# A squared-ReLU MLP whose first product, too, is made of seven products of quarters

## The chip, the cores and the metric

One core of a Trainium2 chip runs the whole program. The metric is the device time of one execution in microseconds (us). TensorE is PE in the profile, VectorE DVE, ScalarE ACT, GpSimd POOL and SyncE SP; nearly all transfers are issued on SP, in program order.

## What is computed

Two layers of an encoder act on 1088 tokens of width 1024 (1024 of a prompt, 64 of a sample). Each layer has a mixer, a cross attention into 256 memory tokens, and an MLP, all with a root-mean-square norm ahead:

```
def rmsnorm(x, g):
    y = x32 * lax.rsqrt(jnp.mean(x32 * x32, axis=-1, keepdims=True) + EPS) * g
def cross_attn(h, mk, mv, w_q, w_o):        # 4 heads of 256
    q = (h @ w_q).reshape(B, L, N_MEM_HEADS, MEM_HEAD_DIM)
    pr = jax.nn.softmax(q k / 16);  return (pr v) @ w_o
def sq_relu_mlp(h, w_up, w_down):           # w_up 1024x4096, w_down 4096x1024
    return jnp.square(jax.nn.relu(h @ w_up)) @ w_down
...
x = x + cross_attn(rmsnorm(x, norm_cross[layer]), ...)
x = x + sq_relu_mlp(rmsnorm(x, norm_mlp[layer]), w_up[layer], w_down[layer])
```

## The kernel before

Tokens lie along the columns, features along the 128 partitions. They are two streams, s = 0 with 512 tokens and s = 1 with 576. All products are made to nearly fp32 accuracy from parts: each operand is split into a rounded high part and the low rest (`split`, L233/L236 and L186/L187: ACT rounds, DVE subtracts), and a product is three matmuls for each block of 128 rows: low times high, high times low, high times high. Weights come in blocks of 128 x 1024 (512 KB): SP loads one into a staging tile `st` (three of them, L174), ACT and DVE split it into `wp` (or `wd` in the second MLP product). A block is loaded as soon as a staging tile is free, and that is when the block two or three ahead has been split.

**Cross attention** (`cross`, then `project_back`) runs for s = 0 and then for s = 1: eight weight blocks `mq`, scores and values of four heads j, eight blocks `mo` which are added to x. The norm of the next stage is prepared within it (`prepared`): the squares of x are summed by PE, DVE scales the sum (L315), POOL raises it to the power -1/2 (L316, tile `rc`), and PE transposes `rc` (L326), from which the row `rb` is made. For s = 1 of the cross attention that is the norm of the MLP of s = 0.

**First MLP product** (`mlp_up`): 32 blocks of w_up. For each, three token blocks of 512, 288 and 288 columns get 24 matmuls each on the tokens times g, not yet normalised; DVE applies ReLU and `rb` on reading PSUM (L969), ACT squares into `u`. After two blocks POOL makes four differences of `u` (L992), and `u` with them goes to DRAM.

**Second MLP product** (`mlp_down`) is already seven products of quarters instead of eight: the token operands are those sums of `u`, and the weights are quarters of w_down and four sums of them, `sums`. `weights_sums` makes these during the first product, a sixteenth at a time: two loads of 512 KB into the one tile `quarters` (L943), four POOL additions of 128 x 512 (L947 to L950), a store of 1 MB to DRAM (L955).

In the first product SP and POOL keep the order of the program; elsewhere a scheduler arranges the instructions of each engine at build time. At run time each engine takes its instructions in order, and one that waits holds all that stand behind it.

## Time and profile before

| | us |
|---|---|
| median of 3 runs (lowest, highest) | 2772.16 (2770.36, 2772.91) |
| profiled execution: device time, span of its trace | 2772.14, 2770.3 |
| PE busy in the span | 2712.8 |
| cross attention, first layer, from 424 to 672: PE busy, POOL busy | 247.3, 15.9 of 248 |
| first MLP product, first layer, from 672 to 1053: PE busy, POOL busy | 379.8, 182.1 of 381 |

The second layer has the same stages, from 1776 to 2023 and from 2023 to 2404. Times in a timeline count from the start of the span. Busy PE is time with a matmul under way; PE is busy nearly throughout, so that a stage is as long as its matmuls and their waits. SPq is SP's queue of transfers: the time shown there is that of issuing one, not of the transfer.

### The profile page before, as it was taken

Reading aid. Unit: us, or ns where it says so; the run is one execution under the profiler, and the core shown is the slowest. Engines: PE = TensorE matmul, PEld = TensorE weight load, DVE = VectorE, ACT = ScalarE, POOL = GpSimd, SP = SyncE. Lnnn points to the kernel's source line nnn. Section 1 sums busy time; section 2 is a strip of 40 time slices with the busy share of each in tenths; the row PEclk is TensorE's granted clock in tenths of the full one; section 3 lists DMA queues with packets and bytes.
Section 4 is the critical chain, followed back from the end, with each engine's and each line's share of the span. In section 5 each row is a group of like instructions: output and inputs, shape, how many; then the busy total and the mean of one; then the engine's idle time right before and its main releaser. Section 6 shows DMA issues by size and latency. Waiting matters only on the chain. (4 is left out here: it accounts for less than half of the span.)

```text
span 2770.3 us, 44519 instructions
## 1 busy us (share of the span) xinstructions
PE 2712.8 (98%) x18280; PEld 2535.7 (92%) x18280; DVE 1393.6 (50%) x2328; ACT 1096.1 (40%) x1929; POOL 541.5 (20%) x486
## 2 busy tenths in 40 slices
PE   8999999999999999999999999999999999999998
PEld 7978998899999999999988899989999999999998
DVE  5596766564222226455457558566532222365453
ACT  5574555353221223333337348344432222243334
POOL 3200000000545442000003004000024555500000
PEclk9998999999999999999999999999999999999999
DMA  8722232322666668555421331323236666675452
GB/s 269 232 78 75 69 101 88 101 71 62 206 221 218 213 213 300 189 188 187 127 67 31 80 79 28 96 88 97 64 125 221 215 213 222 251 258 174 178 175 77
DMA packets 364368, 411.90 MB, mean 149 GB/s; under 512 B 45840, under 2 KB 267040, under 8 KB 364164
## 3 DMA queue, kind: packets, MB, share of 16 engines
q1 hardware_dynamic: 355268, 382.00, 41.8%
q0 software_dynamic: 8896, 27.06, 3.0%
q8 instruction: 143, 2.34, 0.4%
q14 instruction: 61, 0.50, 0.1%
HBM read 299.74 MB, written 109.39 MB: 148 GB/s over the span
## 5 line engine op out<-in xcount | busy, mean ns | idle before, releaser
L216 PE MATMUL mm<-hpH,wp 128*128 128x288 f32 (+2 forms) x5952 | 1422.7, 328 | 4.2 <-DVE U L543 2.6
L216 PEld LDWEIGHTS mm<-hpH,wp 128*128 128x128 f32 x5952 | 1015.5, 189 | 83.5 <-DVE U L543 2.9
L216 PE MATMUL mm<-hpL,wp 128*128 128x288 f32 (+2 forms) x2976 | 928.0, 328 | 2.2 <-DVE hpL L291 2.2
L216 PEld LDWEIGHTS mm<-hpL,wp 128*128 128x128 f32 x2976 | 562.3, 189 | 41.5 <-DVE hpL L291 3.1
L186 ACT ACTIVATE wp<-st 128x1024 fp32r<-128x1024 f32 x282 | 297.8, 1058 | 691.7 <-PE mm L216 434.7
L187 DVE TENSOR_TENSOR wp<-st,wp 128x1024 fp32r<-128x1024 f32 x282 | 344.8, 1224 | 271.3 <-ACT wp L186 266.7
L969 DVE SCALAR_TENSOR_TENSOR t<-mm,rb 128x288 f32<-128x288 f32 (+1 forms) x184 | 99.1, 539 | 507.9 <-PE mm L216 507.9
L992 POOL TENSOR_TENSOR u<-u 128x544 f32<-128x544 f32 x128 | 218.6, 1718 | 382.5 <-ACT u L974 380.0
L316 POOL TENSOR_TENSOR rc<-rc,mhalf 128x4 f32<-128x4 f32 (+1 forms) x21 | 23.4, 1122 | 986.9 <-DVE rc L315 986.9
L1041 PE MATMUL s<-uhl,wd 128*128 128x256 f32 x560 | 157.2, 281 | 4.6 <-DVE wd L187 4.6
L972 ACT ACTIVATE u<-t 128x512 f32<-128x512 f32 x64 | 40.4, 632 | 301.4 <-DVE t L969 301.4
L1042 PE MATMUL s<-uhl,wd 128*128 128x256 f32 x560 | 157.1, 281 | 0.0
L236 DVE TENSOR_TENSOR uhl<-ur,uhl 128x1088 fp32r<-128x1088 f32 x112 | 147.0, 1314 | 19.5 <-ACT uhl L233 19.4
L1043 PE MATMUL s<-uhl,wd 128*128 128x256 f32 x560 | 156.7, 280 | 0.0
L233 ACT ACTIVATE uhl<-ur 128x1088 fp32r<-128x1088 f32 x112 | 123.5, 1104 | 56.1 <-DMA ur<-u 54.0
L186 ACT ACTIVATE wd<-st 128x1024 fp32r<-128x1024 f32 x70 | 73.7, 1055 | 176.5 <-PE t L1043 142.8
L216 PE MATMUL s<-hpH,wp 128*128 128x288 f32 (+1 forms) x576 | 141.3, 330 | 0.0
L974 ACT ACTIVATE u<-t 128x288 f32<-128x288 f32 x128 | 55.9, 436 | 144.0 <-DVE t L969 144.0
L1041 PEld LDWEIGHTS s<-uhl,wd 128*128 128x128 f32 x560 | 105.9, 189 | 5.5 <-DVE wd L187 5.5
L1042 PEld LDWEIGHTS s<-uhl,wd 128*128 128x128 f32 x560 | 105.8, 189 | 0.0
L1043 PEld LDWEIGHTS s<-uhl,wd 128*128 128x128 f32 x560 | 105.6, 189 | 0.0
L216 PEld LDWEIGHTS s<-hpH,wp 128*128 128x128 f32 x576 | 98.0, 188 | 8.0 <-ACT hpH L233 0.3
(367 smaller groups left out, 4804.1 us busy)
## 6 DMA issues: line engine op xcount, KB each, us to landing
u<-u SPq DMA_DIRECT2D x32, 1904.0 KB, 6.7
ur<-u SPq DMA_DIRECT2D x112, 544.0 KB, 6.0
st<-in_w_up_dram SPq DMA_DIRECT2D x64, 512.0 KB, 4.2
quarters<-in_w_down_dram SPq DMA_DIRECT2D x64, 512.0 KB, 4.3
sums<-quarters SPq DMA_DIRECT2D x32, 1024.0 KB, 6.5
st<-sums SPq DMA_DIRECT2D x64, 512.0 KB, 5.5
st<-in_w_down_dram SPq DMA_DIRECT2D x48, 512.0 KB, 5.0
st<-in_w_mq_dram SPq DMA_DIRECT2D x32, 512.0 KB, 3.6
```

Source lines behind the costliest of these rows:

```text
L186: act.activation(wt[:, 0], st, AF.Copy)
L187: dve.tensor_tensor(wt[:, 1], st, f32(wt[:, 0]), OP.subtract)
L216: pe.matmul(ps, a, b, start=i == 0, stop=i == len(terms) - 1)
L233: act.activation(h, src, AF.Copy)
L236: dve.tensor_tensor(l, src, f32(h), OP.subtract)
L969: dve.scalar_tensor_tensor(t[:, :bn], ps[:, :bn], 0.0, nm.rb[:, b0:b0 + bn], OP.max, OP.mult)
L972: act.activation(slots[:, :, :256], t.rearrange("p (a b) -> p a b", a=2), AF.Square)
L974: act.activation(slots[:, b0 // 288, 256:], t[:, :bn], AF.Square)
L992: pool.tensor_tensor(u[:, to], u[:, a], u[:, b], OP.subtract)
L1041: pe.matmul(ps, wl, uh, start=first, stop=False)
L1042: pe.matmul(ps, wh, ul, start=False, stop=False)
L1043: pe.matmul(ps, wh, uh, start=False, stop=half == 1 and g == 3 and k == 1)
```

## The change

1. The first MLP product becomes seven products of quarters as well (class `Up`). Sixteen pairs of weight blocks give, for each stream, four quarters of 512 x 128 and three sums of them, and the halves of x give seven operands. A round is one pair of blocks with one stream: seven products of 12 matmuls of 256 columns (s = 0) or 288 (s = 1). There are 18 passes over weight pairs (two pairs are loaded twice) and 32 rounds a layer.
2. The weights' sums are made by POOL in the staging tiles (`weights`, four subtractions or additions of 128 x 512 for a pair), and each of the seven weight operands is split by ACT and DVE.
3. The token operands are normalised first (`operands`: for each stream sixteen DVE multiplications, four differences, seven splits) and stay in SBUF. Those of s = 0 are made during the last projection of the cross attention, those of s = 1 in the first two rounds of the first product.
4. The products are put together by DVE, which reads PSUM (seven additions a round), ACT takes ReLU and the square, POOL makes the four differences into the two single tiles `ss` and `sq`, and three stores a round take the place of the one store of two blocks.
5. `weights_sums` moves into the cross attention: two sixteenths after the scores of each head, in both streams, with its transfers on SP and its POOL work kept in the order of the program. There is still one tile `quarters`.
6. The second product's first weights lie in other tiles (`wd` for key[3] < 5, else `wp`), and its first tokens are loaded during the last round. `dynamic_dma_scratch_size` is halved.

The diff, cut to what the argument follows:

```diff
@@ cross, at the end of each head j
             scores(j)
             load_kv(j + 1, 0, 1)
+            for q in range(2):
+                weights_sums(l, 8 * s + 2 * j + q, p)
...
+    def weights_sums(l, q, p):
+        a = p.tile([128, 4, 512], F32, tag="quarters", name="quarters", bufs=1)
+        keep = tc.keep_in_program_order
+        for i in range(2):
+            keep(nc.sync.dma_start(a[:, 2 * i:2 * i + 2],
+                                   I["w_down"][l][256 * q + 128 * i:256 * q + 128 * i + 128]
+                                   .rearrange("p (h n) -> p h n", h=2)))
+        for to, one, two, op in ((3, 1, 3, OP.add), (1, 0, 1, OP.subtract), (0, 3, 0, OP.subtract),
+                                 (2, 2, 0, OP.subtract)):
+            keep(pool.tensor_tensor(a[:, to], a[:, one], a[:, two], op))
+        keep(nc.sync.dma_start(sums[l][q // 2][:, :, q % 2], a))
...
-    def mlp_up(l, norms, p, outer):
...
+    class Up:
...
+            self.streams = [0, 1, 0] + list(range(2, 16)) + [14]
+            self.rounds = [(0, 0), (1, 0), (1, 1), (2, 1)]
+            for k in range(3, 17):
+                self.rounds += [(k, 0), (k, 1)] if self.streams[k] != 14 else [(k, 0)]
+            self.rounds.append((17, 1))
...
+        def weights(self, w):
...
+            split(self.wp[j][:, 0], self.wp[j][:, 1], src)
+            if name == "A11":
+                pool.tensor_tensor(odd[:, hi], odd[:, lo], odd[:, hi], OP.add)
+                pool.tensor_tensor(odd[:, lo], even[:, lo], odd[:, lo], OP.subtract)
+                pool.tensor_tensor(even[:, lo], odd[:, hi], even[:, lo], OP.subtract)
+            elif name == "A12":
+                pool.tensor_tensor(even[:, hi], even[:, hi], even[:, lo], OP.subtract)
+            elif name == "S3":
+                self.load(k + 1, 0)
...
+            elif name == "S4":
+                self.load(k + 2, 1)
...
+            def finish(r):
...
+                act.activation(u, u, AF.Relu)
+                act.activation(u, u, AF.Square)
+                pool.tensor_tensor(t[0], u[:, 3], u[:, 0], OP.subtract)
+                pool.tensor_tensor(t[2], u[:, 2], u[:, 3], OP.subtract)
+                pool.tensor_tensor(t[1], u[:, 2], t[0], OP.subtract)
+                pool.tensor_tensor(t[3], t[1], u[:, 1], OP.subtract)
...
+            def hook(i):
+                r, m = up.slots[i]
+                if i == 3:
+                    nm1.columns()
+                elif i == 5:
+                    nm1.rows()
+                    for _ in operands(1, g, nm1, raw1, ops[1], operand):
+                        pass
```

**Three places in the order.** POOL, first layer, the end of the cross attention of s = 1, before (`kvst` are loads of memory keys and values, `o32` a sum of a head's outputs, `rc_6230` the power of the MLP norm of s = 0):

```order
L784 DMA kvst_5767<-kT0_3_801 128x512
L787 DMA kvst_5806<-in_cache_mem_v_dram 128x2x256
L787 DMA kvst_5869<-in_cache_mem_k_dram 128x2x256
L900 TENSOR_TENSOR o32_5798<-o32_5798 128x2x64
L784 DMA kvst_5944<-v0_3_867 128x512
L787 DMA kvst_6066<-in_cache_mem_v_dram 128x2x256
L900 TENSOR_TENSOR o32_6058<-o32_6058 128x2x64
L316 TENSOR_TENSOR rc_6230<-rc_6230,mhalf_107 128x4
L900 TENSOR_TENSOR o32_6175<-o32_6175 128x2x64
```

The same place after the change (L948 is the additions of `weights_sums`, L322 the power, now of `rc_6338`):

```order
L908 TENSOR_TENSOR o32_5894<-o32_5894 128x2x64
L792 DMA kvst_6056<-v0_3_867 128x512
L795 DMA kvst_6178<-in_cache_mem_v_dram 128x2x256
L948 TENSOR_TENSOR quarters_5974<-quarters_5974 128x512 x4
L948 TENSOR_TENSOR quarters_5982<-quarters_5982 128x512 x4
L908 TENSOR_TENSOR o32_6170<-o32_6170 128x2x64
L948 TENSOR_TENSOR quarters_6240<-quarters_6240 128x512 x2
L322 TENSOR_TENSOR rc_6338<-rc_6338,mhalf_107 128x4
L948 TENSOR_TENSOR quarters_6240<-quarters_6240 128x512 x2
L908 TENSOR_TENSOR o32_6303<-o32_6303 128x2x64
L985 TENSOR_TENSOR rd_6375<-rb_6374,ra_6373 128x1024
L948 TENSOR_TENSOR quarters_6248<-quarters_6248 128x512 x4
```

The power stood behind loads and small sums; now fourteen sixteenths and half of the fifteenth stand ahead of it (`rd` belongs to the operands of s = 0). The other power within the cross attention, of the norm of s = 1, has five sixteenths ahead of it. On PE, the transposes of `rc_6338` had 342 matmuls of `mo` behind them before the first product, and now have 363.

SP, the same stretch, before (the last blocks of w_mo, then those of w_up):

```order
L174 DMA st_6021<-in_w_mo_dram 128x8x128
L174 DMA st_6295<-in_w_mo_dram 128x8x128
L174 DMA st_6352<-in_w_mo_dram 128x8x128
L174 DMA st_6409<-in_w_mo_dram 128x8x128
L174 DMA st_6466<-in_w_up_dram 128x8x128
```

And after (L942 loads two halves of a sixteenth, L949 stores its sums, L173 and L1033 load weights):

```order
L173 DMA st_6133<-in_w_mo_dram 128x8x128
L942 DMA quarters_5982<-in_w_down_dram 128x1024 x2
L173 DMA st_6431<-in_w_mo_dram 128x8x128
L949 DMA sums0_6_90<-quarters_5982 512x1x512
L942 DMA quarters_6240<-in_w_down_dram 128x1024 x2
L949 DMA sums0_7_91<-quarters_6240 512x1x512
L942 DMA quarters_6248<-in_w_down_dram 128x1024 x2
L173 DMA st_6496<-in_w_mo_dram 128x8x128
L949 DMA sums0_7_91<-quarters_6248 512x1x512
L173 DMA st_6560<-in_w_mo_dram 128x8x128
L1033 DMA st_6746<-in_w_up_dram 128x8x128
```

The sixteenths follow one another, each load behind the store of the one before, since they share a tile; the loads of weights stand among them. The first sixteenth's loads come right behind the seventh block of `mq` of s = 0.

DVE in the first two rounds of the first product, before (L187 splits a weight block, L969 takes a product):

```order
L969 SCALAR_TENSOR_TENSOR t_6864<-s_6839,rb_6757 128x288
L969 SCALAR_TENSOR_TENSOR t_6892<-s_6867,rb_6757 128x288
L187 TENSOR_TENSOR wp_6951<-st_6637,wp_6951 128x1024
L969 SCALAR_TENSOR_TENSOR t_6920<-s_6895,rb_6757 128x288
L969 SCALAR_TENSOR_TENSOR t_6948<-s_6923,rb_6757 128x288
```

And after (L966, L986, L989 and L239 with a name such as `T2` make operands of s = 1; L239 with `wp` splits a weight operand; L1081 and L1090 put products together):

```order
L966 SCALAR_TENSOR_TENSOR rb_6902<-x1_7_128,gcol_109,rb_7003 128x288
L986 TENSOR_TENSOR rc_6900<-rb_6902,rc_6900 128x1152
L1081 TENSOR_TENSOR uC_6907<-s_7050,uC_6907 128x256
L989 TENSOR_TENSOR ra_6901<-rc_6900,rb_6902 128x1152
L239 TENSOR_TENSOR T2_6904<-rc_6900,T2_6904 128x1152
L239 TENSOR_TENSOR B21_6906<-rb_6902,B21_6906 128x1152
L239 TENSOR_TENSOR T1_6905<-rc_6900,T1_6905 128x1152
L1090 TENSOR_TENSOR uC_6907<-uC_6907,t_6910 128x256
L239 TENSOR_TENSOR wp_6812<-st_6750,wp_6812 128x512
L1081 TENSOR_TENSOR uC_6907<-s_7075,uC_6907 128x256
L239 TENSOR_TENSOR T4_7041<-ra_6901,T4_7041 128x1152
L239 TENSOR_TENSOR wp7_6360<-st_6875,wp7_6360 128x512
```

The splits of the last two weight operands of the second pass (`wp_6812`, `wp7_6360`) now have sixteen multiplications, three differences and five splits of operands, the last `T4`, ahead of them.

## Rows read from the trace of the kernel before

**Rows 1.** The page, busy time of the engines (share of the span, instructions).

```profile
PE 2712.8 (98%) x18280; PEld 2535.7 (92%) x18280; DVE 1393.6 (50%) x2328; ACT 1096.1 (40%) x1929; POOL 541.5 (20%) x486
```

**Rows 2.** Busy time by stretch; then granted clock, DMA share, GB/s.

```profile
424.00:672.00 248.00, 247.34 (x1569) 225.68 (x1568) 150.22 (x273) 113.89 (x231) 15.88 (x25) 1.00 0.29 85
672.00:1053.00 381.00, 379.80 (x2318) 348.61 (x2317) 97.85 (x140) 85.86 (x138) 182.08 (x123) 1.00 0.60 208
2410.00:2414.00 4.00, 4.00 (x23) 4.00 (x22) 0.00 (x0) 0.00 (x0) 3.92 (x4) 0.57 0.60 209
```

**Rows 3.** Timeline of PE, second layer: start, duration, engine, line, tiles, idle before.

```profile
2022.86 0.39 PE L216 MATMUL mm<-hpL,wp 128*128 128x512 f32 x1
...
2404.13 0.28 PE L1041 MATMUL s<-uhl,wp 128*128 128x256 f32 x1
...
2406.87 0.28 PE L1043 MATMUL s<-uhl,wp 128*128 128x256 f32 x1
2409.56 0.39 PE L1041 MATMUL s<-uhl,wp 128*128 128x256 f32 x1 [2.41 <-DVE wp L187]
```

**Rows 4.** Timeline of PE in the second product, 288 columns.

```profile
1103.08 0.29 PE L1041 MATMUL t<-uhl,wd 128*128 128x288 f32 x1
...
1106.25 0.29 PE L1041 MATMUL t<-uhl,wd 128*128 128x288 f32 x1
```

**Rows 5.** Timelines of POOL, SP and DVE over one unit of sums.

```profile
964.25 1.37 POOL L992 TENSOR_TENSOR u<-u 128x544 f32<-128x544 f32 x1
965.58 1.29 POOL L947 TENSOR_TENSOR quarters<-quarters 128x512 f32<-128x512 f32 x1
...
969.67 1.28 POOL L950 TENSOR_TENSOR quarters<-quarters 128x512 f32<-128x512 f32 x1
972.54 2.06 POOL L992 TENSOR_TENSOR u<-u 128x544 f32<-128x544 f32 x1 [1.59 <-ACT u L974]
...
973.97 0.52 SPq L955 DMA_DIRECT2D sums<-quarters  x1
980.15 0.82 SPq L943 DMA_DIRECT2D quarters<-in_w_down_dram  x2
...
972.16 1.22 DVE L187 TENSOR_TENSOR wp<-st,wp 128x1024 fp32r<-128x1024 f32 x1 [0.56 <-ACT wp L186]
```

**Rows 6.** The page's DMA issues (us to landing), and waits of SP's queue.

```profile
quarters<-in_w_down_dram SPq DMA_DIRECT2D x64, 512.0 KB, 4.3
sums<-quarters SPq DMA_DIRECT2D x32, 1024.0 KB, 6.5
st<-in_w_mq_dram SPq DMA_DIRECT2D x32, 512.0 KB, 3.6
...
SPq L943 <- DMA sums<-quarters: 169.3, 28, 7.5
```

**Rows 7.** Timelines of SP, POOL and PE, cross attention of the first layer.

```profile
422.24 0.37 SPq L174 DMA_DIRECT2D st<-in_w_mq_dram  x1
...
492.05 1.57 POOL L316 TENSOR_TENSOR rc<-rc,mhalf 128x4 f32<-128x4 f32 x2 [1.07 <-DVE rc L315]
...
624.92 1.04 POOL L316 TENSOR_TENSOR rc<-rc,mhalf 128x4 f32<-128x4 f32 x1 [12.71 <-DVE rc L315]
...
672.25 0.39 PE L216 MATMUL mm<-hpL,wp 128*128 128x512 f32 x1
```

**Rows 8.** Timelines of SP and POOL, cross attention of the second layer.

```profile
1773.06 0.37 SPq L174 DMA_DIRECT2D st<-in_w_mq_dram  x1
...
1975.53 1.03 POOL L316 TENSOR_TENSOR rc<-rc,mhalf 128x4 f32<-128x4 f32 x1 [12.71 <-DVE rc L315]
```

**Rows 9.** DVE by line and form, 424:672: count, busy, mean ns, idle before.

```profile
L187 DVE TENSOR_TENSOR wp<-st,wp 128x1024 fp32r<-128x1024 f32 x30 | 36.8, 1225 | 14.4 <-ACT wp L186 14.4
...
L813 DVE SCALAR_TENSOR_TENSOR q<-mm,rb 128x288 f32<-128x288 f32 x16 | 7.3, 455 | 12.6 <-PE mm L216 12.4
...
L236 DVE TENSOR_TENSOR hpL<-o,hpH 128x64 fp32r<-128x64 f32 x8 | 1.4, 216 | 0.0
```

More of the change, by code (lines that the diff above doesn't have):

```diff
@@ L119, in plan_mlp @@
     def plan_mlp(l):
-        for n in range(NFF):
-            plan.append(((("up", l), n), "n", cols(I["w_up"][l], n * 128, 128)))
+        stops.append(len(plan))
         w = I["w_down"][l]
@@ L192, in ahead @@
         def ahead(self, n=2):
-            while self.split < min(self.used + n, len(plan)):
+            while self.split < min(self.used + n, self.stop):
                 while self.load():
                     pass
-                if plan[self.split][1] == "s" and plan[self.split][0][3] >= 3 and self.more is None:
+                if plan[self.split][1] == "s" and self.more is None:
                     return
@@ L277, in __init__ @@
             self.count = 0
-            self.pair = Pair() if pair else None
+            self.pair = Pair() if pair and not plain else None
             self.out = None if pair else [hpp.tile([128, 4, NT2], F32, tag="hp", name="yT") for _ in range(2)]
-            if pair:
+            if pair or plain:
                 self.ss = nrm.tile([128, NT2], F32, tag="ss", name="ss", bufs=1)
@@ L287, in chunk @@
             g = gcol[:, c, self.g:self.g + 1]
-            if self.pair is not None:
+            if self.plain:
+                pass
+            elif self.pair is not None:
                 h, l = self.pair.at(c, 0, n)
@@ L755, in drain, with project_back @@
                 self.step()
-    def project_back(s, key, pair, queue=None, order=None, spare=0):
+    def project_back(s, key, pair, queue=None, order=None, spare=0, then=None):
         for n in range(8):
@@ L768, in project_back @@
                 queue.step(2)
+            if then is not None:
+                then(n)
     def cross(l, s, norm, p, then):
@@ L922, in cross @@
         then()
-        project_back(s, ("mo", l, s), o, order=[range(6), range(6, 8)], spare=4 - 2 * s)
+        return dict(s=s, key=("mo", l, s), pair=o, order=[range(6), range(6, 8)], spare=4 - 2 * s)
+    def weights_sums(l, q, p):
[9 more added lines that the diff above has]
+        keep(nc.sync.dma_start(sums[l][q // 2][:, :, q % 2], a))
     def load_u(us, p, m, g):
@@ L999, in mlp_down, with operands, scaled, parts @@
-    def mlp_down(l, us, first, last, p, outer):
-        W.more = p
+    def operands(s, g, nm, raw, ops, alloc):
+        h = WIDTH[s] // 2
+        def scaled(dst, k0, t):
+            for c in range(4):
+                dve.scalar_tensor_tensor(dst[:, c], x[s][k0 + c][:, t * h:t * h + h], gcol[:, k0 + c, g:g + 1],
+                                         nm.rb[:, t * h:t * h + h], OP.mult, OP.mult)
+        def parts(b):
+            if b not in ops:
+                ops[b] = alloc(b)
+            split(ops[b][:, 0], ops[b][:, 1], raw[b])
+        scaled(raw["B11"], 0, 0)
+        yield
+        scaled(raw["B12"], 0, 1)
+        yield
+        dve.tensor_tensor(raw["T1"], raw["B12"], raw["B11"], OP.subtract)
+        parts("B11")
+        yield
+        scaled(raw["B22"], 4, 1)
+        yield
+        scaled(raw["B21"], 4, 0)
+        yield
+        pool.tensor_tensor(raw["T3"], raw["B22"], raw["B12"], OP.subtract)
+        dve.tensor_tensor(raw["T2"], raw["B22"], raw["T1"], OP.subtract)
+        parts("T2")
+        yield
+        dve.tensor_tensor(raw["T4"], raw["T2"], raw["B21"], OP.subtract)
+        for b in ("B21", "T1", "T4", "B22", "T3"):
+            parts(b)
+            yield
@@ L1003, in mlp_down @@
+    def mlp_down(l, us, ready, last, p):
         steps = [(m, h) for m in range(7) for h in range(2)]
-        ready = {(0, g): t for g, t in enumerate(first)}
         banks = {}
@@ L1048, in mlp_down @@
                         g = 4 * after[1] + c
-                        ready[after[0], g] = load_u(us, outer, after[0], g)
+                        ready[after[0], g] = load_u(us, p, after[0], g)
                     if end:
                         next(finish, None)
-        W.more = None
     class Window:
@@ L1368, in attend, with prepared @@
                     self.step(t)
-    def prepared(s, g):
-        norm = Norm(s, g)
+    def prepared(s, g, plain=False):
+        norm = Norm(s, g, plain=plain)
         for c in range(KC):
```

280 lines of the change are left out of this document (194 added, 86 removed).

## The prediction

> **What bounds the kernel now.** I read the busy times first: PE works for 2712.8 us of the span [rows 1], so only fewer or shorter matmuls shorten the kernel, and any wait of PE lengthens it. Then the stretches: in the first MLP product PE is busy for 379.8 of 381 us at full clock; in the cross attention for 247.3 of 248 us, while POOL has 15.9 us of work there and DMA runs at 85 GB/s against 208 [rows 2]. Then the timelines, for the pace of a matmul and for what stands ahead of the two POOL powers (L316) in the cross attention, because PE waits for them in order.
>
> **The first product itself.** It takes 381.3 us, from 2022.86 to 2404.13 [rows 3]. After the change it has 16 pairs x 7 products x 12 matmuls = 1344 matmuls of 256 columns and 1344 of 288. Their pace is read from the second product, which has both: 23 steps from 2404.13 to 2406.87 are 0.119 us each [rows 3], 24 steps from 1103.08 to 1106.25 are 0.132 us [rows 4]. 1344 x 0.251 = 337 us.
>
> The other engines' work of one pair is to fit into 7 x 12 x 0.251 = 21.1 us. On DVE that is seven weight splits of half a 1224 ns split (L187) and fourteen additions of 455 ns (like L813) [rows 9], 10.7 us. On POOL it is four additions of 128 x 512 at 1.34 us [rows 5] and eight of half that width, 10.7 us. Both are hidden if their order lets them, which is the second rival below.
>
> The start is not hidden. The operands of s = 1 are made on DVE in the first two rounds, which have only products of s = 0. Up to the last weight split of the second round they are sixteen multiplications of 288 columns at 0.455 us, and three differences and five splits of 1152 columns at 1.224 x 1152/1024 = 1.38 us: 7.3 + 11.0 = 18.3 us [rows 9], with some 10 us of weight splits and additions between them. They begin when the norm of s = 1 is there, about 6 us into the stage. So that split ends 34 to 36 us in, while PE wants it before its fourteenth product, 13 x 12 x 0.119 = 18.6 us in. The wait is 10 to 20 us; I take 16. Product: 337 + 16 = 353 us, **28 us less per layer**.
>
> **The sums of w_down in the cross attention.** What they leave, the first product's POOL, was hidden there, so their removal brings nothing. What they enter is a chain. One unit before: both loads have landed 0.4 + 4.3 = 4.7 us after the first is issued [rows 6]; four additions take from 965.58 to 970.95; the store is issued at 973.97, and the next load leaves SP at 980.15, when the store has landed, 6.2 us later [rows 5]; the median store takes 6.5 us, and SP has waited for these stores 28 times [rows 6]. The next unit cannot overlap, for there is one tile. So a unit takes 4.7 + 5.4 + 6.2 to 6.5 = 16.3 to 16.6 us; I take 16.5.
>
> POOL beside DVE is slower: the L992 at 964.25 takes 1.37 us, the one at 972.54, beside an L187 of DVE on two SBUF inputs, 2.06 us [rows 5]. In the cross attention DVE groups with two SBUF inputs, ten from L187 (36.8 us) to the last (1.4 us) [rows 9], take 84 of 248 us, a third. Four additions that each lose 0.7 us in a third of the cases lose 0.9 us; as some fall into pauses of DVE, I take 0.4, hence **16.9 us a unit** (from 15.5, if nothing is lost and a store lands a microsecond sooner in the emptier stage, to 17.6).
>
> The Trainium skill (SBUF — State Buffer, section "SBUF: two separate sides") calls the port pair of GpSimd and DVE an exclusive lock, held for the whole instruction. The trace agrees in the two L992 above; by the lock alone every meeting would cost, some 0.9 us a unit, and the sum below would be about 2822.
>
> The first unit's load is issued behind the seventh mq block, at 422.6 [rows 7]. Unit k is then issued at 422.6 + 16.9 (k - 1). The order of POOL has two places where this matters:
> - The power for s = 1 stands behind the fifth unit's additions: 422.6 + 67.6 + 4.7 + 5.4 = 500.3 against 492.05 [rows 7]. PE is held by some 8 us. This is no cost of its own: the chain doesn't wait for PE, and PE meets it again at the next place.
> - The power for the MLP norm stands behind half of the fifteenth unit. It ends at 422.6 + 14 x 16.9 + 4.7 + 2.7 + 1.0 = 667.6, against 624.92 + 1.04 = 626.0 before [rows 7]: 41.6 us late. All of PE's remaining matmuls of mo queue behind its transposes. From that power to the first product it is 46.3 us now (672.25) [rows 7], and 21 more matmuls of 0.132 us make it 49.1: the first product begins at 716.7, 44.4 us later.
>
> The second layer is alike: 1773.06 to 1975.53 between the same two points is 202.5 us, as 422.24 to 624.92 is [rows 8, 7]. The clock falls after such a wait: behind the 2.4 us wait at 2409.56 the granted clock was 0.57 for four microseconds [rows 3, 2], about the lower level of 1.2 GHz, which costs some 1.7 us. I add 0.6, as the transposes and a few matmuls fill part of it: **45 us more per layer**. Weight blocks that stand behind units on SP still come in time: the seventh of mo follows the sixteenth unit's load at 422.6 + 15 x 16.9 = 676, and PE wants it six blocks after the power, past 700.
>
> **The start of the second product.** Its first operands are split behind the last round's work on DVE. Before, this place costs a wait of 2.4 us [rows 3] and a few more behind it; I add 1 us, from nothing to 5.
>
> **The sum.** Per layer -28 + 45 + 1 = +18, two layers +36. The profiled execution took 2772.1 us, the median of the runs is 2772.16, so the same: **2808 us**.
>
> **The rivals.**
> - *The chain is not late, and the fewer matmuls remain: faster.* POOL and DMA are nearly idle in the cross attention [rows 2], and a mq block lands in 3.6 us [rows 6]. If a store took no longer than the 1 MB of both loads, 4.7 us, a unit would be 14.8 us, the power 638.2, the first product 15 us late, a layer 12 us shorter: 2748. The point that decides is 15.6 us a unit, where 14 units save the 18 us. Against it: the median of the stores is 6.5 us over the whole program [rows 6]. 12 in 100. The Trainium skill (DMA: Bandwidth & Descriptors, section "Anatomy of one DMA — SWDGE (gpsimd) path") has 2.0 us and bytes/436 GB/s for a transfer, an estimate of 4.4 us for 1 MB either way; the store's 6.2 us disagrees, and by the page the end would be at about 2732.
> - *The first product is slowed all along.* `ss` and `sq` are single, so POOL's differences of a round wait until the three stores of the round before have landed, and the weight sums stand behind them on POOL. Stores are issued in the middle of the following round, some 5.7 us in, and land 6 to 7 us later: 12.4 us, against the 10 to 11 us of a round and the 2 us for ReLU and square. If this comes short by 1.5 us a pair, 15 pairs lose 20 us a layer: 2848. 14 in 100.
> - *POOL loses most of its meetings with DVE.* At 17.6 us a unit the power is late by ten microseconds more: 2828. 6 in 100.
> - *No change*, at 15.5 to 15.7 us a unit: 6 in 100.
>
> That the change does not do what it says can be left out: the order shows it on every engine.
>
> **Numbers.** The forecast has 62 in 100, with a range of its own from 2785 to 2830. Within 0.2% (5.5 us, about what a measurement of this kernel can tell from no change) 6 in 100; slower 62 + 14 + 6 = 82; faster 12. The range from 2768 takes in a unit of 15.5 us, to 2850 the slowed product; most of the faster case and the end of the slowed one are left out.
>
> **What would show it.** Right: PE waits at the transposes of `rc` for 25 to 45 us near 640 to 670 and again in the second layer, with POOL's additions of `quarters` waiting for loads ahead of it; the first product lasts about 353 us with a wait of 10 to 20 us some 18 us in; SP waits for stores of `sums` about 15 times in each cross attention. Wrong: units shorter than 15.6 us, or a first product that is longer than 365 us, or waits in each of its rounds.

## The result, and the profile after

| | before | after |
|---|---|---|
| median of 4 runs each (lowest, highest), us | 2771.26 (2767.77, 2772.91) | 2889.73 (2889.41, 2891.41) |
| after / before, 95% interval | | 1.043 (1.0412, 1.0449) |
| first layer, first product begins | 672.25 [rows 7] | 732.42 |
| second layer, first product begins | 2022.86 [rows 3] | 2146.61 |
| first layer, first product lasts, up to the second's first matmul | 381.3 | 380.5 |
| second layer, the same | 381.3 | 378.4 |
| second product, first and second layer | 346.3, 347.2 | 341.2, 344.1 |

The change costs 118 us where the forecast had 36. The cross attention is 60 us longer in the first layer and 68 us in the second, which begins 56 us later (1832.2 for 1776.0) and ends 124 us later; the first product, which should have paid for a part of it, gives back 1 and 3 us, and the second product 5 and 3.

The page after, span and busy times, which answers to [rows 1]:

```profile
span 2888.2 us, 47649 instructions
PE 2680.4 (93%) x19048; PEld 2547.6 (88%) x19048; DVE 1693.6 (59%) x2844; ACT 1247.5 (43%) x2113; POOL 772.2 (27%) x762
```

PE works 32 us less than before, and waits for 208 us of the span instead of 58. Two stretches of the first layer, the cross attention and the first product, in the columns of [rows 2]:

```profile
424.00:732.00 308.00, 258.24 (x1555) 231.71 (x1554) 187.02 (x290) 114.61 (x229) 114.79 (x93) 0.93 0.54 171
732.00:1113.00 381.00, 349.58 (x2709) 345.58 (x2707) 213.74 (x382) 160.19 (x233) 209.96 (x196) 0.97 0.43 134
```

In the first, PE waits for 50 of 308 us, where before it was 0.7 of 248. What PE waited for there (total us, times, longest):

```profile
PE t L867 <- DVE pr L856: 18.9, 6, 10.5
PE mm L219 <- DVE q L821: 13.7, 4, 4.1
PE t L332 <- POOL rc L322: 7.5, 1, 7.5
PE mm L219 <- DVE x L771: 4.0, 4, 2.8
```

No row names a weight split (`wp`): PE did not wait for weight blocks here. Most rows name DVE, which is not the cause of the longest waits. The timelines of POOL, ACT, DVE and PE around the longest wait, one after the other:

```profile
660.26 5.28 POOL L948 TENSOR_TENSOR quarters<-quarters 128x512 f32<-128x512 f32 x4 [11.72 <-DMA quarters<-in_w_down_dram]
665.51 0.45 POOL L908 TENSOR_TENSOR o<-o 128x128 f32<-128x128 f32 x1
675.22 2.65 POOL L948 TENSOR_TENSOR quarters<-quarters 128x512 f32<-128x512 f32 x2 [9.26 <-DMA quarters<-in_w_down_dram]
677.83 1.04 POOL L322 TENSOR_TENSOR rc<-rc,mhalf 128x4 f32<-128x4 f32 x1
...
665.99 0.40 ACT L236 ACTIVATE hpH<-o 128x64 fp32r<-128x64 f32 x2 [10.81 <-POOL o L908]
...
666.28 0.37 DVE L239 TENSOR_TENSOR hpL<-o,hpH 128x64 fp32r<-128x64 f32 x2 [10.57 <-ACT hpH L236]
...
668.64 1.09 PE L867 MATMUL t<-ident,pr 128*128 128x128 f32 x4 [10.47 <-DVE pr L856]
678.92 0.32 PE L332 MATMUL t<-ident,rc 128*128 128x128 f32 x1
```

Read from the top: POOL waits 11.7 us for a load of `quarters`; a sum of a head's outputs, 0.45 us long, stands behind the four additions; ACT waits 10.8 us for that sum, DVE 10.6 us for ACT, and PE 10.5 us for DVE's next work, `pr`. Then the fifteenth unit comes, and the power of the MLP norm behind half of it ends at 678.87, before it was 625.96 [rows 7]. PE's transposes of `rc` follow without a wait, since the chain had held PE already; the 7.5 us at L332 are those of the earlier power, at 503. Waits for `q` can have the same source: at 559.61 PE has waited 3.3 us for DVE, DVE 5.1 us for ACT, and ACT 6.7 us for a load of memory values that left POOL at 553.58, behind the eighth unit's additions.

The loads of the one tile, first layer (SP's issues: count, ns, first and last start):

```profile
L942 SPq DMA_DIRECT2D quarters<-in_w_down_dram x32: 328/424/1527, 420.7 to 687.0; - x32
```

The timeline of SP around the ninth unit, with a split on ACT and DVE:

```profile
541.46 0.82 SPq L942 DMA_DIRECT2D quarters<-in_w_down_dram  x2
553.66 0.52 SPq L949 DMA_DIRECT2D sums<-quarters  x1
554.27 10.25 SPq L173 DMA_DIRECT2D st<-in_w_mq_dram  x4
564.57 1.04 SPq L942 DMA_DIRECT2D quarters<-in_w_down_dram  x2
...
561.81 1.06 ACT L185 ACTIVATE wp<-st 128x1024 fp32r<-128x1024 f32 x1 [3.58 <-DMA st<-in_w_mq_dram]
...
562.90 1.23 DVE L186 TENSOR_TENSOR wp<-st,wp 128x1024 fp32r<-128x1024 f32 x1 [3.34 <-ACT wp L185]
```

From the first unit's loads to the sixteenth's, at 686.6, it is 265.9 us, 17.7 us a unit. The eighth takes 23.1: the ninth's loads stand on SP behind four weight loads. The last of the four leaves at 564.15, when DVE has freed a staging tile with the split at 562.90. That split waits through ACT for a block whose load had itself left SP only behind the eighth unit's store, at 554.27. The first product in slices of 20 us:

```profile
752.00:772.00 20.00, 9.42 (x64) 9.21 (x63) 16.92 (x24) 8.51 (x9) 9.32 (x5) 0.69 0.12 30
...
812.00:832.00 20.00, 20.00 (x162) 20.00 (x161) 9.91 (x19) 7.99 (x13) 11.42 (x11) 1.00 0.39 118
...
1072.00:1092.00 20.00, 16.14 (x116) 15.93 (x115) 10.77 (x21) 8.67 (x13) 11.68 (x12) 0.91 0.33 108
1092.00:1112.00 20.00, 14.79 (x107) 14.09 (x106) 13.86 (x21) 10.25 (x13) 8.10 (x8) 0.98 0.61 195
```

A full slice has 162 matmuls, 8.1 per us. The four slices up to 812 have 468, worth 57.8 of 80 us: 22 us lost. The twelve up to 1052 have 1903, 5 us lost; the rest, up to 1113, 378, 14 us lost. Without the 41 to 42 us lost the product would last some 339. What PE waited for in the first 80 us, and from 1052 to the second product's first matmul:

```profile
PE s L219 <- DVE wp L239: 12.3, 2, 10.6
PE t L332 <- POOL rc L322: 3.1, 1, 3.1
...
PE s L1257 <- ACT uhl L236: 5.0, 1, 5.0
PE s L219 <- DVE wp L239: 4.9, 3, 3.9
```

The 5.0 us are the wait for the second product's first tokens (`uhl`), which lies ahead of its first matmul and so within the 380.5.

### The profile page after: what moved, and what is told of

Its sections match the earlier page's. It is cut to its first block, busy times and chain, and to the rows that moved or that the text cites. A ratio compares the mean times of both kernels' runs of the same rounds, so it can differ in the third digit from the quotient of the medians.

```text
span 2888.2 us, 47649 instructions
## 1 busy us (share of the span) xinstructions
PE 2680.4 (93%) x19048; PEld 2547.6 (88%) x19048; DVE 1693.6 (59%) x2844; ACT 1247.5 (43%) x2113; POOL 772.2 (27%) x762
## 5 line engine op out<-in xcount | busy, mean ns | idle before, releaser
L219 PE MATMUL mm<-hpH,wp 128*128 128x288 f32 (+3 forms) x3008 | 731.8, 330 | 42.4 <-DVE q L821 27.6
L219 PEld LDWEIGHTS mm<-hpH,wp 128*128 128x128 f32 x3008 | 518.8, 190 | 86.3 <-DVE q L821 29.8
L219 PE MATMUL mm<-hpL,wp 128*128 128x288 f32 (+3 forms) x1504 | 473.4, 330 | 2.3 <-DVE hpL L297 2.2
L239 DVE TENSOR_TENSOR wp<-st,wp 128x512 fp32r<-128x512 f32 x252 | 215.9, 865 | 251.4 <-ACT wp L236 249.3
L219 PE MATMUL s<-T,wp 128*128 128x288 f32 (+1 forms) x2304 | 312.5, 294 | 37.0 <-DVE wp L239 36.7
L219 PEld LDWEIGHTS s<-T,wp 128*128 128x128 f32 x2304 | 301.2, 193 | 42.5 <-DVE wp L239 42.0
L219 PEld LDWEIGHTS mm<-hpL,wp 128*128 128x128 f32 x1504 | 288.8, 192 | 21.4 <-DVE hpL L297 3.2
L948 POOL TENSOR_TENSOR quarters<-quarters 128x512 f32<-128x512 f32 x128 | 182.0, 1422 | 347.6 <-DMA quarters<-in_w_down_dram 340.2
L322 POOL TENSOR_TENSOR rc<-rc,mhalf 128x4 f32<-128x4 f32 (+1 forms) x21 | 22.4, 1076 | 850.4 <-DVE rc L321 850.4
L219 PE MATMUL mm<-B,wp 128*128 128x256 f32 (+1 forms) x1536 | 204.6, 288 | 4.1 <-DVE wp L239 4.1
L219 PEld LDWEIGHTS mm<-B,wp 128*128 128x128 f32 x1536 | 197.2, 188 | 5.3 <-DVE wp L239 5.3
L239 DVE TENSOR_TENSOR uhl<-ur,uhl 128x1088 fp32r<-128x1088 f32 x112 | 143.9, 1286 | 17.8 <-ACT uhl L236 17.6
L1081 DVE TENSOR_TENSOR uC<-s,uC 128x256 f32<-128x256 f32 (+1 forms) x320 | 133.5, 432 | 11.6 <-PE s L219 5.0
```

What stands on the lines that cost most here:

```text
L219: pe.matmul(ps, a, b, start=i == 0, stop=i == len(terms) - 1)
L239: dve.tensor_tensor(l, src, f32(h), OP.subtract)
L322: pool.tensor_tensor(rc[:m, b0:b1], rc[:m, b0:b1], mhalf[:m, b0:b1], OP.pow)
L948: keep(pool.tensor_tensor(a[:, to], a[:, one], a[:, two], op))
L1081: dve.tensor_tensor(to, b, a, op)
```

## The experiments

Three explanations stood against one another for the 118 us: the chain (additions wait on POOL for loads, and short work that PE needs waits behind them), the transfers themselves, and the additions' own work, on POOL and beside DVE. For the first product the question was why it saved nothing. All medians, and ratios to runs of the kernel before on the same chip; not all kernels ran on one chip, so that differences of a few us between them show nothing:

| kernel | median, us | ratio (95%) |
|---|---|---|
| sums_alone | 2881.78 | 1.0399 (1.0381, 1.0417) |
| no_sums | 2757.10 | 0.9953 (0.9937, 0.9968) |
| no_adds | 2759.16 | 0.9966 (0.9949, 0.9982) |
| adds_only | 2795.84 | 1.0087 (1.0064, 1.011) |
| o32_dve | 2881.03 | 1.0396 (1.0379, 1.0412) |
| half_tiles | 2833.72 | 1.0218 (1.0192, 1.0244) |
| spread | 2824.43 | 1.0199 (1.0178, 1.022) |
| spread_kv | 2819.54 | 1.0175 (1.016, 1.019) |
| spread_sp | 2789.94 | 1.0069 (1.005, 1.0089) |
| spread_act | 2780.48 | 1.0037 (1.0022, 1.0051) |
| dve_adds | 2807.91 | 1.0128 (1.0103, 1.0153) |
| elsewhere | 2823.00 | 1.0183 (1.0167, 1.0198) |
| elsewhere_end | 2801.90 | 1.0112 (1.0097, 1.0127) |
| spread_start | 2825.10 | 1.02 (1.0182, 1.0218) |
| spread_end | 2808.15 | 1.0135 (1.011, 1.016) |
| no_sums_end | 2735.07 | 0.9875 (0.9851, 0.9899) |

### Which part costs

**sums_alone** is the kernel before with nothing but the move of `weights_sums` into the cross attention.

```diff
@@ cross, end of head j, in the kernel before
+            for q in range(2):
+                weights_sums(l, 8 * s + 2 * j + q, p)
@@ mlp_up
-            weights_sums(q)
```

> The kernel before with only weights_sums moved into the cross attention; the first product stays 32 blocks with the tokens scaled behind it. If what stands behind the units on POOL and SP costs the time (theory A), the cross attentions are 60 and 66 us longer, as in the changed kernel (678.9 to 732.4 in place of 626.0 to 672.3 at the end), and the kernel takes 2771 + 126 = about 2895 us. If the lengthening needs the new first product, whose operands are made in the last projection (theory B), it is at most the 45 us per layer of the power alone, some 2860, or near nothing.

The move alone costs 111 us. POOL at the end of the first layer's cross attention:

```profile
672.54 5.39 POOL L939 TENSOR_TENSOR quarters<-quarters 128x512 f32<-128x512 f32 x4 [9.07 <-DMA quarters<-in_w_down_dram]
677.88 1.04 POOL L316 TENSOR_TENSOR rc<-rc,mhalf 128x4 f32<-128x4 f32 x1
```

The same power, within 0.1 us of the same time as in the changed kernel: the new first product has no part in its lateness.

**no_sums** is the changed kernel without `weights_sums`; **no_adds** keeps its loads and stores, but not the additions; **adds_only** makes the additions on one cleared tile and keeps no transfer.

```diff
@@ no_sums (adds_only has the first of these edits too)
-                    src = sums[l][g][:, q]
+                    src = dram(w, 4 * g * 128 * D + q % 2 * 512, [[D, 128], [256 * D, 2], [1, 512]])
-            for q in range(2):
-                weights_sums(l, 8 * s + 2 * j + q, p)
@@ no_adds, in weights_sums
-        for to, one, two, op in ((3, 1, 3, OP.add), (1, 0, 1, OP.subtract), (0, 3, 0, OP.subtract),
...
-            keep(pool.tensor_tensor(a[:, to], a[:, one], a[:, two], op))
@@ adds_only, in weights_sums
-        a = p.tile([128, 4, 512], F32, tag="quarters", name="quarters", bufs=1)
+        if q == 0:
+            still[l] = p.tile([128, 4, 512], F32, tag="quarters", name="quarters", bufs=1)
+            pool.memset(still[l], 0.0)
+        a = still[l]
-            keep(nc.sync.dma_start(a[:, 2 * i:2 * i + 2],
...
-        keep(nc.sync.dma_start(sums[l][q // 2][:, :, q % 2], a))
```

> The changed kernel without weights_sums; the second product reads quarters of w_down where it should read their sums, so four of its seven weight operands are wrong, with as many loads and matmuls. Theory A: the cross attentions are as long as before but for a few us at their end (the x additions that wait beside the operands), the first product keeps its waits at the start and the end and gains nothing: 2889.7 - 2 x 58 = about 2770 to 2780 us. If the waits in the first product follow from the late cross attention (theory B), they fall away here too and the kernel takes about 2720 us.

> The changed kernel whose units load and store without the four additions between, so that the sums are plain quarters and the output is not the reference's. The transfers, their order on SP and the traffic stay, at some 11 us a unit; POOL has nothing that waits ahead of the powers, the o32 additions and the loads of keys and values. Theory A (what stands behind the additions on POOL costs the time): the cross attentions are at most 5 to 15 us longer than before, 2757 + 2 x 10 = about 2777 us. Rival (the transfers on SP hold the weight blocks, or the traffic holds the loads): above 2830 us.

> The changed kernel with the 64 additions of a layer kept at the end of each head on POOL, but on one tile that is cleared once: they wait for no load, and nothing is loaded or stored for them (the second product reads quarters of w_down where it should read their sums). Theory A (POOL's waits for transfers, with what is queued behind them): near the run without sums, 2757 to 2772 us. Rival (theory C: the additions themselves, which slow DVE and POOL beside each other and which the powers and loads stand behind, cost the time): 2800 us or more.

Between the changed kernel and no_sums lie 132.6 us. The transfers alone bring 2 of them, which is within the noise. The additions alone, which wait for no load, bring 39, where at most 15 were expected. The other 92 arise only where additions wait for loads: the chain. The windows of no_adds and of adds_only over the cross attention show the two ends, DMA at 217 GB/s with PE busy for 246.6 of 248 us in the one, PE at 234.3 in the other:

```profile
424.00:672.00 248.00, 246.55 (x1554) 224.12 (x1553) 164.90 (x292) 114.90 (x229) 22.93 (x29) 1.00 0.66 217
```

adds_only:

```profile
424.00:672.00 248.00, 234.33 (x1459) 211.36 (x1458) 181.60 (x280) 111.45 (x223) 91.94 (x74) 1.00 0.27 79
```

Part of the 39 us is DVE. Its groups by form, 424 to 672 (count, busy us, mean ns, idle before), in no_sums:

```profile
L856 DVE TENSOR_SCALAR pr<-pr,sm 128x256 f32<-128x256 f32 x32 | 9.8, 346 | 0.3
L239 DVE TENSOR_TENSOR ql<-q,qh 128x288 fp32r<-128x288 f32 x16 | 7.3, 454 | 2.7 <-ACT qh L236 2.6
L821 DVE SCALAR_TENSOR_TENSOR q<-mm,rb 128x288 f32<-128x288 f32 x16 | 7.3, 455 | 12.7 <-PE mm L219 12.5
L239 DVE TENSOR_TENSOR tp<-t,tp 128x512 fp32r<-128x512 f32 x16 | 10.3, 682 | 0.6 <-ACT tp L236 0.6
```

The same groups in adds_only:

```profile
L856 DVE TENSOR_SCALAR pr<-pr,sm 128x256 f32<-128x256 f32 x32 | 16.5, 557 | 0.3
L239 DVE TENSOR_TENSOR ql<-q,qh 128x288 fp32r<-128x288 f32 x16 | 14.5, 906 | 2.9 <-ACT qh L236 2.9
L821 DVE SCALAR_TENSOR_TENSOR q<-mm,rb 128x288 f32<-128x288 f32 x16 | 7.3, 455 | 8.8 <-PE mm L219 8.5
L239 DVE TENSOR_TENSOR tp<-t,tp 128x512 fp32r<-128x512 f32 x16 | 10.2, 679 | 0.6 <-ACT tp L236 0.6
```

Beside POOL's additions two groups that read only SBUF rise on average (`ql` 454 to 906 ns, `pr` 346 to 557), and those with an operand in PSUM (`mm`, `t`) stay as they were. The rise is that of a few operations: the median of `pr` is 347 ns in no_sums and 346 in adds_only, its longest 496 and 2026. The Trainium skill (SBUF — State Buffer, section "SBUF: two separate sides") has an exclusive lock, held for a whole instruction, between GpSimd and DVE operations that have two SBUF inputs or run in a two-port mode. These rows agree: `ql` has two SBUF inputs, the groups with an operand in PSUM have one. `pr` is held too; that it runs in such a mode is not shown.

### Is it the chain

**o32_dve** takes the sums of a head's outputs off POOL, **half_tiles** halves the unit and has two tiles, and **spread** has three half tiles, loads two units ahead, and a unit at each of several places of a head and of `project_back`.

```diff
@@ o32_dve
-                pool.tensor_tensor(o32[:, :, 0], o32[:, :, 0], o32[:, :, 1], OP.add)
+                dve.tensor_tensor(o32[:, :, 0], o32[:, :, 0], o32[:, :, 1], OP.add)
@@ half_tiles
-        a = p.tile([128, 4, 512], F32, tag="quarters", name="quarters", bufs=1)
+        a = p.tile([128, 4, 256], F32, tag="quarters", name="quarters", bufs=2)
@@ spread, class Sums
+            a = self.p.tile([128, 4, 256], F32, tag="quarters", name="quarters", bufs=3)
...
+            while len(self.tiles) < min(32, self.n + 3):
+                self.load()
@@ cross, project_back
+            ws.make()
```

> The changed kernel with only the small addition o32, for which PE waited 10.8 us in the last head (657.9 to 668.6), on DVE; the power of the MLP norm stays behind half of the fifteenth unit, and the chain of units with it. If the chain sets the end, as predicted, PE now comes earlier to the transposes of rc, waits there for the power at about 678, and the time is within 6 us of 2890. If the small waits added up to the 60 us (rival), the 10.8 us and the shorter ones behind o32 go in both layers: 2860 us or less.

> The changed kernel with the sums made in units of half the size in two tiles of half the size, the loads one unit ahead; POOL's work stays, its order too. Theory A with the transfers as the cause of the chain: a half unit then takes little more than the landing of its store, about 5 us, 10 in place of 17.8 us for a sixteenth, so that the last power is no longer late and the cross attentions are 5 to 15 us longer than before, not 63: 2889.7 - 2 x 52 = about 2785 us. Rival: POOL's additions beside DVE, or the order itself, cost the time whatever the transfers take: above 2850 us.

> The changed kernel with all its additions, in half units in three half tiles, set one by one between the halves of the queries, the heads and, for the first stream, the blocks of mo; a half unit's loads are issued two half units ahead, so that POOL finds its data landed. POOL has the same work, DMA the same bytes as in the run half_tiles (2834 us). Theory A: POOL no longer waits, and the cross attentions end within 5 to 10 us of the run without sums: 2765 to 2780 us. Rival (POOL's additions themselves, beside DVE, or their transfers slow the stage): 2820 us or more.

o32_dve gains only 9 us. One wait goes, and PE meets the chain at the next place, the power:

```profile
681.00 1.12 PE L332 MATMUL t<-ident,rc 128*128 128x128 f32 x4 [13.30 <-POOL rc L322]
```

No run has the powers off POOL too, so what they cost there by themselves is open.

half_tiles gains 56 us, about half of what was expected, as a half unit still takes some 7 us: SP itself is held, for 99.7 us by stores of `sums` between 424 and 680. Its timeline, where the next store stands behind a load that waits for the store before:

```profile
479.84 1.22 SPq L944 DMA_DIRECT2D quarters<-in_w_down_dram  x2
483.14 0.56 SPq L955 DMA_DIRECT2D sums<-quarters  x1
486.80 1.20 SPq L944 DMA_DIRECT2D quarters<-in_w_down_dram  x2
```

spread gains 65 us, where 110 to 125 were expected; it lies where the rival was put. One thing that is left is the order of POOL, now the other way round: additions stand behind a load of memory values that waits 22 us for DVE. They pile up from 494 to 543, and the next load of values leaves behind them at 543.11. ACT waits 12.9 us for that, DVE 11.6 us for ACT, and PE for DVE. POOL, and PE's wait:

```profile
491.34 0.72 POOL L795 DMA_DIRECT2D kvst<-in_cache_mem_v_dram  x1 [22.44 <-DVE v L239]
...
550.36 0.61 PE L219 MATMUL mm<-hpH,wp 128*128 128x288 f32 x1 [8.14 <-DVE q L821]
```

### Other places for the loads, the additions and the sums

All but elsewhere also leave out the single passes at the first product's end (spread_end, below), which are worth 16 us in spread. On top of spread, three have the head sums on DVE: **spread_kv** keeps the `kvst` loads on POOL in program order, **spread_sp** issues them on SP, **spread_act** on ACT (the latter two with the first head of s = 1 begun within the projection of s = 0). **dve_adds** makes the additions of w_down's sums on DVE. **elsewhere** takes the sums out of the cross attention: the first layer's are made in its mixer, the second layer's during the first layer's second product; **elsewhere_end** is the same without the single passes.

```diff
@@ spread_sp (spread_act: act.dma_start)
-                    pool.dma_start(st, kvd[l, which, j])
+                    tc.keep_in_program_order(nc.sync.dma_start(st, kvd[l, which, j]))
@@ dve_adds
-            keep(pool.tensor_tensor(a[:, to], a[:, one], a[:, two], op))
+                dve.tensor_tensor(a[:, to], a[:, one], a[:, two], op)
@@ elsewhere, second product
+                    if l == 0 and turn > 8 and turn % 8 < 6:
+                        ws.make()
@@ elsewhere, mixer
-            project_back(0, ("out", 0), mx.y[0], q)
+            project_back(0, ("out", 0), mx.y[0], q, then=ws.make)
```

> As spread_end (2808 us), with the loads of memory keys and values kept in the order of the program among the half units, and o32 on DVE. In spread POOL stood still for 22 us (469 to 491) behind such a load, which waited for its tile, and the half units of the first stream slid into the second. If that is where the rest of the time went (theory A again, with another waiting instruction), the cross attentions end within 10 us of the run without sums: 2808 - 2 x 20 = about 2765 us or less, at or below the kernel before. Rival: the additions cost time wherever they stand, by holding DVE; above 2795 us.

> As spread_end (2808 us), with the loads of memory keys and values on SP in the order of the program, those of the second stream's first head issued during the first stream's blocks of mo, and o32 on DVE: on POOL only the additions and the two powers are left. Theory A: no load waits behind an addition; 2745 to 2770 us, faster than the kernel before. Theory C: above 2790 us, with PE waiting for DVE all over the stage. A third way: SP's queue holds keys, values and weight blocks instead, with single waits of PE of 5 us or more, and 2780 us or more.

> As spread_sp (2790 us), with the loads of memory keys and values issued by ACT, where PE waited 3.1, 8.0, 2.4 and 1.2 us for them on SP in each layer. If those waits are SP's order, they go: 2790 - 2 x 12 = about 2766 us, no slower than the kernel before. Rival: ACT, which splits what it has just loaded, waits for the landing itself and holds what stands behind it: no gain or a loss.

> As spread_end (2808 us), with the additions of the sums on DVE in place of POOL: DVE gets 128 operations of 256 columns more in each layer, some 0.42 us each, 54 us, beside the 165 of 248 us that it is busy in the run without sums; POOL has none. If the additions cost through POOL and DVE holding each other and through POOL's queue, both are gone, and the cross attentions are at most 10 us longer than without sums: 2735 + 20 = about 2755 us, faster than the kernel before. Rival: DVE's own queue now waits for the loads, with the splits and products' results behind it: 2790 us or more.

> The changed kernel with all sums, made where POOL has next to nothing that PE waits for: those of the first layer in the mixer ahead (half units in three half tiles), those of the second layer in the first layer's second product (quarter units, 128 columns, in three tiles of 2 KB a partition), loads two units ahead. Theory A: nothing stands ahead of the powers and the loads in the cross attentions, which are as in the run without sums: 2757 to 2770 us. Rival: the 67 MB of loads and stores among the weight blocks on SP, or the additions beside a second product where DVE is half busy, give back as much: 2790 us or more.

> As elsewhere, without the second pass over pair 14 at the end of the first product. In the cross attention's spread version that gave 16 us (2824 to 2808 us) where 12 to 16 were expected. If those were the waits of two passes of one round each, the same 12 to 16 us come off here: 2742 to 2757 us, faster than both kernels. If the 16 us came from the changed cross attention or by chance, nothing does.

spread_kv misses: against spread_end it is 11 us slower, and PE now waits 9.0 us, up to 547.8, for a memory load that stands behind half units. With these loads off POOL the kernel comes to 2789.94 and 2780.48, the best with all sums, but 20 and 14 us above what was expected. The longest wait of spread_act is again one for DVE:

```profile
598.68 0.47 PE L872 MATMUL t<-ident,pr 64*128 64x64 f32 x2 [9.45 <-DVE tp L239]
```

dve_adds misses by 53 us and equals spread_end (2807.91 and 2808.15): DVE's own order then waits for the loads as POOL's did, 36.8 us in 23 waits between 424 and 700. elsewhere misses too, and elsewhere_end with it, though it is 21 us below elsewhere. Its cross attention is as clean as that of no_sums, but the sums cost as much where they went. The windows of the mixer and of the second product of the first layer, in elsewhere:

```profile
140.00:370.00 230.00, 202.97 (x1056) 176.11 (x1055) 191.44 (x316) 124.87 (x158) 126.21 (x124) 0.93 0.65 201
1080.00:1440.00 360.00, 337.71 (x2620) 335.39 (x2618) 185.63 (x199) 121.03 (x124) 186.21 (x261) 0.96 0.83 260
```

The same two stretches in no_sums:

```profile
140.00:340.00 200.00, 190.84 (x1034) 168.15 (x1033) 153.33 (x312) 122.42 (x155) 5.42 (x3) 0.97 0.26 76
1050.00:1380.00 330.00, 329.16 (x2622) 328.14 (x2621) 174.49 (x200) 119.36 (x123) 3.46 (x5) 1.00 0.53 183
```

Each stretch is 30 us longer for about the same matmuls. In the mixer DVE is busy for 191 us instead of 153, and PE waits for it; in the second product DMA is at 0.83 of its time and PE waits 12.9 us for the splits of tokens that land late.

### The first product

**spread_start** spreads the operands of s = 1 over the first rounds, one at a time; **spread_end** drops the two single passes at the end, so that each pair but those of the start is loaded once for both streams; **no_sums_end** is no_sums with the same end.

```diff
@@ spread_start, hook
-                    for _ in operands(1, g, nm1, raw1, ops[1], operand):
+                if 5 <= i < 14:
+                    next(make1, None)
...
+                elif i == 14:
+                    for _ in make1:
                         pass
@@ spread_end, no_sums_end
-            self.streams = [0, 1, 0] + list(range(2, 16)) + [14]
+            self.streams = [0, 1, 0] + list(range(2, 16))
...
-                self.rounds += [(k, 0), (k, 1)] if self.streams[k] != 14 else [(k, 0)]
-            self.rounds.append((17, 1))
+                self.rounds += [(k, 0), (k, 1)]
```

> As spread, with the operands of s = 1 made step by step between products 5 and 14, the weight splits among them, and POOL's difference T3 behind DVE's T4, which it held for 3.5 us. If the wait of 8 to 11 us about 24 us into the first product is due to the order on DVE, it shrinks by 4 to 6 us a layer: 8 to 12 us less than spread. Rival: DVE is simply full there (40 us of work against 20 us of products), the wait moves to the third round, and the time stays within 4 us.

> As spread, without the second pass over pair 14 at the end: 17 passes, the last two rounds being both streams of pair 15. If the waits near the end of the first product (1.7, 4.2, 0.7 and 1.1 us in the run without sums) come from two passes of one round each, whose weights must be summed and split in 10 us instead of 21, they go: 12 to 16 us less than spread over both layers. Rival: the second product then begins with a longer wait, since its first weights and tokens come later, and the time stays within 4 us of spread or rises.

> The run without sums (the second product reads quarters of w_down where it should read their sums) and without the second pass over pair 14. What the first product is worth by itself, without its last single pass: if the 16 and 21 us that this edit gave in two other kernels are the product's own, 2757 - 18 = about 2739 us; if they came with those kernels' cross attentions, 2750 us or more.

spread_start gains nothing. PE in the first rounds shows one long wait cut into several:

```profile
741.96 0.61 PE L219 MATMUL mm<-B,wp 128*128 128x288 f32 x1 [4.03 <-ACT B L236]
743.85 3.01 PE L219 MATMUL mm<-B,wp 128*128 128x288 f32 x11 [1.28 <-DVE B L239]
...
763.90 6.56 PE L219 MATMUL s<-T,wp 128*128 128x288 f32 x36 [2.46 <-DVE wp L239]
```

Two orders give the same time, as they would if the work were too much for these rounds; no run has less of it there. The end is another matter: spread_end is 16 us faster than spread, no_sums_end 22 us faster than no_sums, in two layers. The first product of no_sums in the first layer, in a window:

```profile
671.00:1049.00 378.00, 350.96 (x2707) 347.88 (x2705) 215.51 (x381) 160.78 (x233) 207.19 (x196) 0.97 0.43 134
```

The same of no_sums_end:

```profile
669.00:1032.00 363.00, 346.51 (x2706) 343.73 (x2706) 206.09 (x367) 154.72 (x224) 200.40 (x192) 0.98 0.43 137
```

The 15 us contain the wait for the second product's first tokens, 4.5 us in no_sums and none in no_sums_end. Some 4 us come back as waits within the second product, and the program keeps 11 us a layer.

## Why the prediction was wrong in size

**Right.** The sign and the place. The move of `weights_sums` costs more than the first product gives; the power of the MLP norm is late behind the fifteenth unit (sums_alone, o32_dve). Twelve of the fourteen units before it take 17.1 us, for which I took 16.9, and the power for s = 1 begins at 501.9, for which I had 500.3, and PE waits for it for 7.5 us, for which I had 8. Seven products cost PE what was worked out: without its losses the first product would have lasted some 339 us by the slices above, for which I had 337.

**Step "unit k is issued at 422.6 + 16.9 (k - 1)": 45 us a layer became 60 and 68.** It let the chain run by itself ("the chain doesn't wait for PE"). The forecast asked whether weight blocks come late behind units on SP, and not whether units come late behind weight blocks. The eighth and ninth units took 23.1 and 20.5 us. In the eighth, the ninth's loads stood behind four blocks of `mq`, which waited for a staging tile; in the ninth, its additions began 6.8 us after the loads were issued instead of 4.7, and the next loads left 7.7 us after its store instead of 6.2 to 6.5. SP's waits name DVE and a load there; that PE's own lateness had a part is not shown. The power ended 11.3 us later than forecast, and from there to the first product it was 53.5 us instead of 49.1, with three waits for DVE's additions to x. In the second layer the power came 17.6 us later after the first load than forecast, and the rest took 5 us more. That PE would wait 25 to 45 us at these transposes was wrong too: it came to them without a wait, having waited ahead of them at places that I had not looked up, behind the head sums of L908 and the loads of memory values.

**Step "28 us less per layer": 1 and 3.** The wait at the start was the only loss that I counted, 16 us. The waits of the first 80 us come to 16.8, but that the numbers meet is partly luck. The weight split for which PE waits came 35 us in, as forecast; PE came to it after 25 us and not after 18.6, and waited 10.6. Another 3.9 us are waits for the norm of s = 1, the power on POOL and its row, for which the sum had nothing. The slices show 42 us lost: 22 in the first 80 us (the waits, and the clock behind them, 0.69 granted between 752 and 772), 5 in the middle, where six waits of 0.7 us at most are for weight splits, and 14 at the end, 5.0 of them for the second product's tokens. The end is shown by no_sums_end, the product 15 us shorter. Passes of one round need a new set of seven weight operands for every 84 matmuls, where the forecast gave DVE and POOL two rounds. I had read the table of rounds and not asked how often weights are made in its last passes. What holds PE in the middle was not tried.

**Step "start of the second product", +1.** Its first wait is 5.0 and 4.5 us and lies ahead of its first matmul; before, the waits were 5.6 and 3.9 us within it. The product itself is 5 and 3 us shorter, so that the place costs nothing in the first layer and 1 us in the second, about as forecast. Counted without this wait the first product is 6 and 7 us shorter than before.

**The rivals.** "POOL loses most of its meetings with DVE" had the port right and the victim wrong. The additions took 1.42 us each, close to the forecast's, and DVE paid: additions that wait for nothing cost 39 us in the two layers. The forecast had no term for what POOL does to DVE. "The first product is slowed all along" gave 20 us a layer by stores; the loss is 26 us over the forecast, but at its start and its end. The fit that the prediction sets against the store's 6.2 us stands in the Trainium skill (DMA: Bandwidth & Descriptors, section "Anatomy of one DMA — SWDGE (gpsimd) path") for transfers issued on POOL; these are issued on SP, and no run here has such a store on POOL.

Without any sums of w_down, which the kernel before does make, no_sums has 13 us less than it by the ratio, and no_sums_end 35. None of the places tried for the sums left any of that; whether another would is open.

## What to carry to other kernels

A queue with idle time is not free time. POOL had 232 of 248 us idle, and of the 133 us that the units cost, 92 arise because they wait in order ahead of short work that others need; before work with waits goes to an idle engine, list every instruction behind each wait and who needs it. A chain that alternates loads and stores on one queue also waits for whatever stands between them, here weight loads that need a staging tile. And of a table of rounds, price the ends as well as the body: the two single passes gave back 15 of the 42 us that the product's fewer matmuls saved (381 to 339), 11 of them for the whole program.

## What was not expected of the hardware

DVE, beside POOL's additions, took 906 instead of 454 ns on average for a subtraction of 128 x 288 from SBUF, and 557 instead of 346 ns for a multiplication of 128 x 256 by a column, of which most kept their time and the longest took 2026 ns. POOL's addition of 128 x 512 went from 1.31 us on average in the kernel before to 1.54 us in the window of adds_only. Transfers were the cheap part: 64 MB of loads and stores more than doubled the traffic of the cross attention (80 GB/s in no_sums, 217 in no_adds), and cost no more than the noise.
